# A hybrid encoder trunk: low parts of the mixers' weights read back from DRAM, the first weights in quarters beside x, and the mixer's steps in another order

## The chip, the cores and the metric

The kernel runs on one core of a Trainium2 chip. A time is the device time of one execution in microseconds (us). TensorE (PE) multiplies matrices, VectorE (DVE), ScalarE (ACT) and GpSimd (POOL) work on elements, and SyncE (SP) issues most of the DMAs. Each engine runs its own queue of instructions in order and waits for the others by semaphores.

## What is computed

x is 512 tokens of 1024 features, all float32. Two layers, each a half-step feed-forward, a mixer with three groups of heads, and another half-step feed-forward:

```python
for i in range(DEPTH):                       # DEPTH = 2
    x = x + 0.5 * swiglu(rmsnorm(x, ffn1_norm[i]), ffn1_w_gate[i], ffn1_w_up[i], ffn1_w_down[i])
    h = rmsnorm(x, mix_norm[i]) @ w_in[i]
    y_mla = mla_mixer(h[..., OFF_Q:OFF_KV], h[..., OFF_KV:OFF_KPE], h[..., OFF_KPE:OFF_CONV], ...)
    y_conv = conformer_conv_mixer(h[..., OFF_CONV:OFF_HY], ...)    # gate, 31 taps, layer norm, silu
    y_hy = hyena_mixer(h[..., OFF_HY:], ...)                       # short taps, two long convolutions by DFT
    y = concat([rmsnorm(y_mla, g[:e1]), rmsnorm(y_conv, g[e1:e2]), rmsnorm(y_hy, g[e2:])])
    x = x + y @ w_out[i]
    x = x + 0.5 * swiglu(rmsnorm(x, ffn2_norm[i]), ffn2_w_gate[i], ffn2_w_up[i], ffn2_w_down[i])
return rmsnorm(x, final_norm)
```

mla_mixer is latent attention with 8 heads: queries from a normalised 256-wide latent, keys and values from a 128-wide one, a rotary key of 32 features that all heads share, softmax over 512 keys.

## The kernel before

Everything is kept with features on the 128 partitions and the 512 tokens in the free dimension; x is eight such tiles. A float32 product is made of three passes on operands split into a high part (rounded to fp32r) and a low part (the rest): high x high, high x low, low x high. For a weight tile of 128 x 1024 this takes one load, a cast on ACT for the high part (a_copy, L360) and a subtraction for the low part (e_tt, on DVE at L371 or on POOL at L373), all in load_w; then 24 matmuls of 512 columns (mm3, L417 to L419). The raw, the high and the low part each take one of 13 buffers of 128 x 1024 (WBUFS, tag "w"). In the mixer four of these hold the tables of the long convolution's DFT.

The stages are: ffn, the first layer's first feed-forward (to about 395 us); the first mixer (to about 650 us); ffn_seven, the second feed-forward and the next layer's first one (other products, L692 to L694, with 256 columns); the second mixer (about 1332 to 1590 us); and a last ffn_seven. Between the tiles of ffn, pump calls a filler, early: rotary tables and the spectra of the long convolutions' filters for both layers, step by step; the second layer's spectra go to DRAM ("kept").

In the mixer, MIX_ORDER lists the steps: C (a projection pair of the gated convolution), A and B (its taps, one DVE operation each, on two halves of the channels), H (projections of the long convolution's inputs, with three short taps), Y (the ten steps of the two long convolutions), Q, KV and K (latents and the rotary key), W (the latent weights), V, S and P (values, scores and their products for each head), CF and HF (end of the convolution groups), OM and OR (the output projection, its attention half and the rest, eight tiles each; the later one of a tile also starts the next norm). A word's number after A, B, Y is a count. SECOND lists, for each step, which of its free choices (e_tt: DVE or POOL; e_scaled: ACT or POOL) take the second engine.

The kernel is written as a plan: every operation is put into it with an engine, a cost, what it reads and writes. A list scheduler (Plan.issue) then goes through modelled time and gives each free engine its ready operation with the lowest number (the order of the program), as far as buffers are free, tags being given out in the program's order. So the order of the words sets priorities, and the queue of each engine, SP with its loads included, is fixed by modelled time.

At the start, x's tiles come in turn with the parameters of layer 0 (67.5 KB) behind the first; the first weight pair comes in four half tiles (first_half), the first of them behind x[0], the second behind x[3], the others behind all of x. Gate and up products run one after the other over all eight x tiles.

## Time and profile before

| | us |
|---|---|
| three timed runs, median | 1943.11 |
| lowest and highest | 1941.32, 1943.93 |
| the profiled execution | 1942.71 |
| its span, first to last instruction | 1940.6 |

The profile of one execution gives, for every instruction, its engine, its start and length, and what ended the wait before it. A busy PE in it isn't a PE at its peak: matmuls are pipelined, and two that wait for each other can still cover the time between them. So beside the busy time the number of matmuls in a stretch is read, against the pace in a stretch where nothing waits. Over the whole span PE is busy 97%, DVE 78%, ACT 48%, POOL 24%.

### The profile page before, as it was taken

How to read it: one execution, taken by the hardware profiler on the slowest of the kernel's cores; microseconds unless marked ns; L12 is line 12 of the kernel's file. 1: busy time of each engine (PE TensorE's matmuls, PEld its weight loads, DVE VectorE, ACT ScalarE, POOL GpSimd, SP SyncE). 2: the span in 40 equal slices, each digit the busy share in tenths (PEclk: the TensorE clock that was granted, in tenths of full speed). 3: DMA queues.
4: the chain of work that ended last, by engine and by line, in shares of the span. 5: the costliest groups of instructions: out<-in, count | busy, mean ns of one | idle time of the engine just before them, and what ended most of it. 6: DMA issues, size and time to landing. Idle time of an engine off the chain costs nothing.

```text
span 1940.6 us, 28881 instructions
## 1 busy us (share of the span) xinstructions
PE 1890.0 (97%) x11265; PEld 1672.8 (86%) x11265; DVE 1506.1 (78%) x2323; ACT 932.3 (48%) x1533; POOL 465.5 (24%) x410
## 2 busy tenths in 40 slices
PE   9999999997999899999999999999999989999998
PEld 7888888886878899989889998997777879899898
DVE  7655465659998988869798886973899899688684
ACT  6333223433695644525454452543368675345253
POOL 1133103445465201001020000104466521000002
PEclk9999999999999999999999999999999999999999
DMA  6333333432003223323323232343310133323231
GB/s 218 101 102 102 121 109 100 129 113 76 12 17 101 90 88 109 110 87 109 109 88 104 93 120 77 109 153 103 98 33 17 45 104 100 118 87 116 81 131 44
DMA packets 61209, 185.52 MB, mean 96 GB/s; under 512 B 6928, under 2 KB 11024, under 8 KB 61072
## 3 DMA queue, kind: packets, MB, share of 16 engines
q1 hardware_dynamic: 57616, 176.86, 27.4%
q0 software_dynamic: 3456, 6.82, 1.2%
q8 instruction: 88, 1.44, 0.3%
q14 instruction: 49, 0.40, 0.1%
HBM read 179.45 MB, written 4.19 MB: 95 GB/s over the span
## 4 chain that ended last, share of the span: by engine, by line
PE 79%; DVE 9%; ACT 4%; DMA 4%; POOL 2%; issue 2%; POOLq 0%; SPq 0%; ACTq 0%; DVEq 0%
PE ps L419 15%; PE ps L417 15%; PE ps L418 15%; PE ps L692 11%; PE ps L694 10%; PE ps L693 10%; DMA wr<-in_win 1%; DVE ptl L333 1%; ACT wh L360 1%; POOL wl L373 1%; DMA wr<-in_dn 1%; DVE wl L371 1%; PE ps L408 1%; DMA wr<-in_gu 1%; ACT p L355 1%
## 5 line engine op out<-in xcount | busy, mean ns | idle before, releaser
L360 ACT CAST wh<-wr 128x1024 fp32r<-128x1024 f32 (+2 forms) x394 | 392.1, 1000 | 547.0 <-DMA wr<-in_gu 204.0
L371 DVE TENSOR_TENSOR wl<-wr,wh 128x1024 fp32r<-128x1024 f32 (+2 forms) x354 | 443.7, 1255 | 252.2 <-ACT wh L360 220.8
L694 PE MATMUL ps<-xa,wl 128*128 128x256 f32 x1320 | 373.9, 283 | 6.8 <-DVE wl L371 6.8
L692 PE MATMUL ps<-xa,wh 128*128 128x256 f32 x1320 | 374.6, 284 | 4.6 <-ACT wh L360 3.4
L693 PE MATMUL ps<-xa,wh 128*128 128x256 f32 x1320 | 373.5, 283 | 0.0
L373 POOL TENSOR_TENSOR s<-s,rb 128x256 f32<-128x256 f32 (+1 forms) x79 | 97.9, 1242 | 909.0 <-DVE s L333 769.3
L694 PEld LDWEIGHTS ps<-xa,wl 128*128 128x128 f32 x1320 | 253.2, 192 | 7.8 <-DVE wl L371 7.8
L692 PEld LDWEIGHTS ps<-xa,wh 128*128 128x128 f32 x1320 | 253.2, 192 | 7.0 <-ACT wh L360 3.8
L417 PE MATMUL ps<-gh,wh 128*128 128x512 f32 x656 | 255.4, 389 | 0.0
L418 PE MATMUL ps<-gl,wh 128*128 128x512 f32 x656 | 255.4, 389 | 0.0
L419 PE MATMUL ps<-gh,wl 128*128 128x512 f32 x656 | 255.2, 389 | 0.0
L693 PEld LDWEIGHTS ps<-xa,wh 128*128 128x128 f32 x1320 | 253.3, 192 | 0.4
L417 PE MATMUL ps<-xh,wh 128*128 128x512 f32 x544 | 215.1, 395 | 0.0
L418 PE MATMUL ps<-xl,wh 128*128 128x512 f32 x544 | 213.2, 392 | 0.0
L419 PE MATMUL ps<-xh,wl 128*128 128x512 f32 x544 | 212.9, 391 | 0.0
L419 PEld LDWEIGHTS ps<-gh,wl 128*128 128x128 f32 x656 | 123.1, 188 | 25.7
L418 PEld LDWEIGHTS ps<-gl,wh 128*128 128x128 f32 x656 | 123.2, 188 | 25.1
L417 PEld LDWEIGHTS ps<-gh,wh 128*128 128x128 f32 x656 | 123.2, 188 | 24.9
L419 PEld LDWEIGHTS ps<-xh,wl 128*128 128x128 f32 x544 | 103.0, 189 | 21.8
L417 PEld LDWEIGHTS ps<-xh,wh 128*128 128x128 f32 x544 | 103.3, 190 | 21.4 <-issue 0.2
L418 PEld LDWEIGHTS ps<-xl,wh 128*128 128x128 f32 x544 | 103.2, 190 | 21.4 <-issue 0.2
L355 ACT ACTIVATE s<-s 128x512 f32<-128x512 f32 x88 | 55.4, 632 | 128.6 <-DVE s L333 128.6
(305 smaller groups left out, 3915.5 us busy)
## 6 DMA issues: line engine op xcount, KB each, us to landing
wr<-in_gu SPq DMA_DIRECT2D x174, 512.0 KB, 3.6
wr<-in_dn SPq DMA_DIRECT2D x64, 512.0 KB, 3.7
wr<-in_win SPq DMA_DIRECT2D x28, 512.0 KB, 3.5
wr<-in_dn SPq DMA_DIRECT2D x32, 384.0 KB, 3.2
wr<-in_wout SPq DMA_DIRECT2D x32, 256.0 KB, 2.7
dft<-in_dft POOLq DMA_DIRECT2D x8, 448.0 KB, 4.7
x<-in_xT SPq DMA_DIRECT2D x8, 256.0 KB, 6.0
mat<-in_spec POOLq DMA_DIRECT2D x8, 256.0 KB, 3.7
```

Of the source, the lines that this page charges most:

```text
L333: lambda: nc.vector.tensor_tensor(out=g(o), in0=g(x0), in1=g(x1), op=op), rd(x0, x1), [o],
L355: lambda: nc.scalar.activation(g(o), g(x0), func, bias=g(bias), scale=g(scale), **({} if accum is None else {"accum_out": g(accum)})),
L360: plan.add("ACT", 0.06 + o.free * 0.86e-3, lambda: nc.scalar.copy(out=g(o), in_=g(x0)), rd(x0), [o])
L371: lambda: nc.vector.tensor_tensor(out=g(o), in0=g(x0), in1=g(x1), op=op), True),
L373: lambda: nc.gpsimd.tensor_tensor(out=g(o), in0=g(x0), in1=g(x1), op=op), True)],
L408: plan.add("PE", 0.11, lambda: nc.tensor.transpose(g(o), g(x0), g(ident)), [x0, ident], [o])
L417: nc.tensor.matmul(oo, lhsT=h, rhs=x0, start=(i == 0), stop=False)
L418: nc.tensor.matmul(oo, lhsT=h, rhs=x1, start=False, stop=False)
L419: nc.tensor.matmul(oo, lhsT=lo, rhs=x0, start=False, stop=(i == n - 1))
L692: nc.tensor.matmul(oo, lhsT=h, rhs=x0, start=start, stop=False, skip_group_check=more)
L693: nc.tensor.matmul(oo, lhsT=h, rhs=x1, start=False, stop=False, skip_group_check=more)
L694: nc.tensor.matmul(oo, lhsT=lo, rhs=x0, start=False, stop=stop, skip_group_check=more)
```

## The change

- keep_low, new: in the first feed-forward, beside the steps of the filter spectra, one or two weight tiles of the mixers at a time are loaded, split, and their low part is stored to DRAM: 13 of the 14 projection tiles (all but the rotary key's), the 3 latent tiles and the 8 output tiles of both layers, 48 of 512 KB in all.
- load_kept takes the place of load_w in the mixers: raw part and low part are both loaded, and only the cast for the high part is left. The output tiles are read in halves, as before.
- MIX_ORDER and SECOND are new, and BLOCKS and SIDES, the order of the blocks and sides of the long convolutions.
- The first weight pair comes in quarters, each with both gate and up for two of x's tiles, in turn with x; the gate and up products run side by side. The gain of the first norm is loaded by itself (4 KB); the parameters of layer 0 come behind x.

```diff
...
-BLOCKS = ((1, 0), (1, 0))
-SIDES = ((0, 1), (1, 0))
+BLOCKS = ((0, 1), (0, 1))
+SIDES = ((1, 0), (1, 0))
 SEVEN_CHUNKS = ((0, 6), (6, 14), (14, 22))
...
-MIX_ORDER = ("C0 A2 C1 A1 B1 H1 Q A1 B2 H2 H0 B2 A2 B2 A2 B2 Y1 KV K Y1 W H3 B4 A2 S0 B3 A6 S1 B1 H4 B1 H5 A1 B1 "
-             "A2 B2 A1 B2 Y1 B3 S4 Y2 A4 V A2 P4 S2 Y1 B2 A2 S5 B1 Y1 A2 B1 P2 S3 S6 S7 Y1 P0 P1 P3 P6 P5 P7 CF Y1 "
-             "OM0 OM2 Y1 HF OR0 OM4 OM1 OM7 OM5 OM6 OR1 OM3 OR2 OR3 OR4 OR5 OR6 OR7")
-
-SECOND = ("C0:12 K:0 C1:012 Q:134 H1:0 Y0:0123 H5:0 Y1:01347 Y2:01234567 KV:01 H2:0 H4:0 W:012 Y4:0 S2:23 S0:01 "
-          "Y5:012345 S1:012 Y7:0123567 S4:012 S5:4 S3:12 Y6:01234567 P1:0 S6:234 S7:0134 P3:01 P5:01 P7:0 "
-          "CF:0456 OM0:0 OM4:0 HF:01 OM3:0 OR0:0 OM6:0 OR1:467 OR2:03 OR3:0245 OR4:3 OR6:3 OR7:2")
+MIX_ORDER = ("C0 A5 K H0 C1 B1 A1 H1 H2 B1 A2 B1 A2 B2 A1 Y1 A1 KV B1 Q H4 Y1 W S0 B1 H3 A1 Y1 A1 H5 Y1 A2 B2 S2 "
+             "B2 S1 B2 A1 B1 A1 B1 A1 B2 A2 B1 A1 B1 S4 Y2 B1 V P0 B1 P1 A2 P2 A2 B1 P4 B1 A2 S3 A1 B1 A1 B1 Y1 S5 "
+             "B2 S6 S7 B2 Y1 B1 P3 Y1 P6 CF Y1 P5 P7 OM0 OM3 HF OM1 OR0 OM4 OR1 OM2 OR2 OR3 OR4 OM7 OM5 OR5 OM6 "
+             "OR6 OR7")
+
+SECOND = ("C1:0 Q:012 Y0:01235 KV:0 K:0 Y2:0123456 S0:024 S1:123 Y1:0123567 S4:014 Y4:0 Y3:0 S2:03 Y5:01234 "
+          "S5:124 Y7:12457 S3:03 S6:0134 S7:01234 Y6:0127 P3:1 P7:0 CF:023456 Y8:0 Y9:0 OR0:12 OR1:125 OR2:01 "
+          "OR3:456 OR4:012 OR5:356 OR6:2 OR7:347")
 SECOND = {w: set(map(int, n)) for w, n in (t.split(":") for t in SECOND.split())}
 POOL_OUT = (2,)
 SLOTS = 60
...
-    def mm3(o, pairs):
+    def mm3(o, pairs, first=True, last=True):
...
-                nc.tensor.matmul(oo, lhsT=h, rhs=x0, start=(i == 0), stop=False)
+                nc.tensor.matmul(oo, lhsT=h, rhs=x0, start=(first and i == 0), stop=False)
                 nc.tensor.matmul(oo, lhsT=h, rhs=x1, start=False, stop=False)
-                nc.tensor.matmul(oo, lhsT=lo, rhs=x0, start=False, stop=(i == n - 1))
+                nc.tensor.matmul(oo, lhsT=lo, rhs=x0, start=False, stop=(last and i == n - 1))
             return go
 
         for i, p in enumerate(pairs):
...
+    gain = const([P, KD], "gain")
...
     def pc(l, name, i=0, rows=P):
         c = PC[name] + i
+        if (l, name) == (0, "ffn1"):
+            return gain[:, i:i + 1]
         return par[l][:rows, c:c + 1]
 
 
...
+        return hi, lo
+
+    lows = {}
+
+    def keep_low(l, name, i, src):
+
+        raw, hi, lo = wtile("wr", F32), wtile("wh", F32R), wtile("wl", F32R)
+        load(raw, src)
+        a_copy(hi, raw)
+        e_tt(lo, raw, hi.f, ALU.subtract, 0)
+        t = lows[l, name, i] = plan.tile(dram, 32 * depth, "low", (P, 1024), F32, nm("low"))
+        load(t, lo.f)
+
+    def keep_lows(l):
+        for name, n in (("win", 14), ("wkvb", 1), ("wqb", 2), ("wout", KD)):
+            for i in range(n):
+                if name != "win" or i != 7:
+                    yield l, name, i, a[name][l] if name == "wkvb" else a[name][l, i]
+
+    def load_kept(l, name, i, c=slice(0, 1024)):
+
+        n = c.stop - c.start
+        raw, hi, lo = wtile("wr", F32), wtile("wh", F32R), wtile("wl", F32R)
+        src = a[name][l] if name == "wkvb" else a[name][l, i]
+        load(raw[:, :n], src[:, c])
+        load(lo[:, :n].f, lows[l, name, i][:, c])
+        a_copy(hi[:, :n], raw[:, :n])
         return hi, lo
 
     def ktiles(wt, n):
...
-        first_tiles = bool(first)
         for ci, (c0, c1) in enumerate(FF_CHUNKS):
             gh, gl = [], []
             for b in range(c0, c1):
                 p2 = []
-                for j in range(2):
-                    wt = first.pop() if first else load_w(a[f"gu{which}"][l, b, j], 1024)
+                if first and b == 0:
+                    p2 = [ps(), ps()]
+                    first(*p2)
+                for j in range(len(p2), 2):
+                    wt = load_w(a[f"gu{which}"][l, b, j], 1024)
                     p = ps()
                     mm3(p, nrm.pairs(wt))
                     p2.append(p)
                 gh.append(s2(F32R, "gh"))
                 gl.append(s2(F32R, "gl"))
                 held.append((*p2, gh[-1], gl[-1]))
-                if not (first_tiles and b == 0):
+                if not (first and b == 0):
                     for t in held:
                         evac(*t)
                     held.clear()
 
...
-            wt = load_w(a["win"][l, mt], 1024)
+            wt = load_kept(l, "win", mt)
...
-            lat["wkv"] = load_w(a["wkvb"][l], 1024)
-            lat["wq"] = [load_w(a["wqb"][l, k], 1024) for k in range(2)]
+            lat["wkv"] = load_kept(l, "wkvb", 0)
+            lat["wq"] = [load_kept(l, "wqb", k) for k in range(2)]
...
-            wt = load_w(a["wout"][l, d, :, 512:1024], 512)
+            wt = load_kept(l, "wout", d, slice(512, 1024))
...
-            wt = load_w(a["wout"][l, d, :, 0:512], 512)
+            wt = load_kept(l, "wout", d, slice(0, 512))
...
-    halves = [[s2(s="w0"), s2(F32R, "w0h"), s2(F32R, "w0l")] for _ in range(4)]
-
-    def first_half(i):
-        raw, hi, lo = halves[i]
-        load(raw, a["gu1"][0, 0, i // 2, :, (i % 2) * S:(i % 2 + 1) * S])
-        split(raw, hi, lo)
-
+    quarters = []
     load(x[0], a["xT"][0])
-    load(par[0], a["par"][0])
-    first_half(0)
+    load(gain, a["par"][0, :, 0:KD])
     for k in range(KD):
         if k:
             load(x[k], a["xT"][k])
+        if k % 2 == 0:
+            raw, hi, lo = s2(s="w0"), s2(F32R, "w0h"), s2(F32R, "w0l")
+            load(raw.halves(), a["gu1"][0, 0, :, :, k * P:(k + 2) * P].rearrange("j p c -> p j c"))
+            quarters.append((hi, lo))
         nrm.add(k, False)
-        if k == 3:
-            first_half(1)
-    first_half(2)
-    first_half(3)
-    load(cc, a["cc"])
-    load(ident, a["ident"])
-
-    class Halves:
-
-
-        def __init__(self, parts):
-            self.parts = parts
-
-        def __getitem__(self, k):
-            h, c = divmod(k[1].start, S)
-            return self.parts[h][:, c:c + P]
-
-    first = [tuple(Halves([halves[2 * j][i], halves[2 * j + 1][i]]) for i in (1, 2)) for j in (1, 0)]
+        if k % 2 == 0:
+            split(raw, hi, lo)
+    for t, n in ((par[0], a["par"][0]), (cc, a["cc"]), (ident, a["ident"])):
+        load(t, n)
+
+    def first(pg, pu):
+
+        for k in range(KD):
+            hi, lo = quarters[k // 2]
+            for j, p in enumerate((pg, pu)):
+                c = slice(j * 256 + k % 2 * P, j * 256 + k % 2 * P + P)
+                mm3(p, [(hi[:, c], lo[:, c], *nrm.x[k])], k == 0, k == KD - 1)
 
...
-        yield from spectra(0, specs[0])
-        for l in range(1, depth):
-            yield from spectra(l, specs[l])
+        todo = [lw for l in range(depth) for lw in keep_lows(l)]
+        steps = 0
+        for l in range(depth):
+            for _ in spectra(l, specs[l]):
+                steps += 1
+                for _ in range(1 + (steps % 4 != 0)):
+                    if todo:
+                        keep_low(*todo.pop(0))
+                yield 1
+            if l == 0:
+                continue
             for k in range(2):
                 for jb in range(2):
                     for o in range(2):
                         t = plan.tile(dram, 8 * (depth - 1), "kept", (P, S), F32, nm("kept"))
                         load(t, specs[l][k][jb][o])
                         specs[l][k][jb][o] = t
+        while todo:
+            keep_low(*todo.pop(0))
+            yield 1
```

## Rows read from the trace of the kernel before

**Rows 1.** First line of the page: the span.
```profile
span 1940.6 us, 28881 instructions
```
**Rows 2.** Busy time by stretch: from:to, length, engines' busy us (instructions), PEclk, DMA share, GB/s.
```profile
0.00:25.00 25.00, 21.24 (x74) 15.52 (x75) 18.33 (x27) 18.73 (x29) 1.41 (x10) 0.93 0.90 320
...
50.00:395.00 345.00, 345.00 (x1526) 285.38 (x1525) 195.20 (x266) 121.22 (x165) 88.89 (x76) 1.00 0.35 111
395.00:418.00 23.00, 23.00 (x111) 19.16 (x110) 8.96 (x18) 7.25 (x9) 10.68 (x6) 1.00 0.34 113
...
440.00:490.00 50.00, 39.44 (x167) 30.75 (x166) 46.72 (x71) 20.56 (x31) 27.71 (x21) 0.90 0.21 67
490.00:600.00 110.00, 108.05 (x593) 89.75 (x592) 102.72 (x206) 85.29 (x176) 62.06 (x64) 1.00 0.06 20
...
635.00:655.00 20.00, 15.05 (x112) 13.78 (x111) 19.52 (x36) 13.01 (x25) 4.71 (x4) 1.00 0.15 53
1330.00:1356.00 26.00, 23.70 (x102) 19.30 (x102) 5.78 (x9) 6.13 (x8) 12.45 (x8) 0.94 0.25 81
...
1378.00:1427.00 49.00, 42.28 (x181) 33.19 (x180) 46.21 (x73) 21.88 (x31) 29.30 (x21) 0.94 0.20 65
...
1572.00:1592.00 20.00, 15.06 (x109) 13.62 (x108) 19.97 (x38) 12.99 (x26) 4.26 (x5) 1.00 0.15 54
```
**Rows 3.** Waits of PE in the mixers (third of the second): total, times, longest us.
```profile
PE ps L417 <- ACT qh L360: 6.5, 1, 6.5
PE ps L408 <- DVE sq L371: 3.3, 1, 3.3
...
PE ps L408 <- POOL r L390: 2.5, 2, 2.3
```
**Rows 4.** Groups on DVE, 397 to 640 us: xcount | busy us, mean ns | idle before.
```profile
L371 DVE TENSOR_TENSOR wl<-wr,wh 128x512 fp32r<-128x512 f32 x9 | 6.2, 695 | 0.4 <-ACT wh L360 0.4
L371 DVE TENSOR_TENSOR wl<-wr,wh 128x1024 fp32r<-128x1024 f32 x5 | 6.1, 1219 | 5.0 <-ACT wh L360 5.0
...
L371 DVE TENSOR_TENSOR w<-m 128x256 f32<-128x256 f32 x3 | 4.4, 1479 | 0.0
...
L371 DVE TENSOR_TENSOR fold<-ho 128x128 f32<-128x128 f32 x2 | 2.4, 1216 | 0.0
...
L371 DVE TENSOR_TENSOR xr<-xr,xs 128x256 f32<-128x256 f32 x3 | 1.2, 413 | 0.0
```
**Rows 5.** Groups on POOL, 397 to 640 us, same columns.
```profile
L373 POOL TENSOR_TENSOR wl<-wr,wh 128x1024 fp32r<-128x1024 f32 x11 | 26.4, 2397 | 20.1 <-ACT wh L360 19.9 <-issue 0.2
...
L373 POOL TENSOR_TENSOR wl<-wr,wh 128x512 fp32r<-128x512 f32 x7 | 9.5, 1365 | 3.6 <-PE ps L418 3.4 <-issue 0.2
```
**Rows 6.** Timeline, 436 to 441 us: start us, length us, instruction.
```profile
436.44 0.29 DVE L371 TENSOR_TENSOR fold<-ho 128x128 f32<-128x128 f32 x1
...
438.22 2.40 POOL L373 TENSOR_TENSOR wl<-wr,wh 128x1024 fp32r<-128x1024 f32 x1 [6.13 <-ACT wh L360]
...
438.62 2.14 DVE L371 TENSOR_TENSOR fold<-ho 128x128 f32<-128x128 f32 x1
```
**Rows 7.** First feed-forward: DVE group, cast (ns), landing of loads, SP's wait.
```profile
L371 DVE TENSOR_TENSOR wl<-wr,wh 128x1024 fp32r<-128x1024 f32 x49 | 61.8, 1261 | 111.3 <-ACT wh L360 111.3
...
L360 ACT CAST wh<-wr x32: 836/1050/1057, 205.7 to 389.5; 128x1024 fp32r<-128x1024 f32 x24, 128x768 fp32r<-128x768 f32 x8
...
wr<-in_gu SPq DMA_DIRECT2D x31, 512.0 KB, 3.4
...
SPq L398 <- PE ps L419: 108.4, 21, 7.3
```
**Rows 8.** Timeline of the first tile: first matmul, last x tiles, next tile's first.
```profile
7.00 0.50 PE L417 MATMUL ps<-xh,w0h 128*128 128x512 f32 x1 [1.76 <-ACT w0h L360]
...
12.79 1.32 ACT L355 ACTIVATE xh<-x,par 128x512 fp32r<-128x512 f32 x2
...
20.93 0.19 PEld L417 LDWEIGHTS ps<-xh,wh 128*128 128x128 f32 x1
```

## The prediction

> **What bounds the kernel now.** The profiled execution took 1942.71 us, of which 1940.6 us are its span [rows 1]; the median of the three timed runs is 1943.11 us, so the sum below is made against 1942.7 and the 0.4 us between them is ignored. First come the busy times by stretch [rows 2]: the long feed-forward stretches keep TensorE (PE) full. From 50 to 395 us, 1526 matmuls take 345 us, 0.226 us each with nothing between them; I use that as the pace of a 512-column matmul, and one 128x1024 weight tile, 24 of them, is 5.42 us of PE. What PE loses lies in few places. In the first mixer, 440 to 490 holds 167 matmuls, worth 167 x 0.226 = 37.7 us of the 50, so 12.3 us are lost, a part of it to a granted clock of 0.90 behind the gaps. Then 490 to 600 shows 2.0 us idle (the matmuls there are short ones of several widths, so this row understates the loss) and 635 to 655, where the mixer gives over to the next feed-forward, 4.95 us. The second mixer repeats it: 26 - 102 x 0.226 = 2.9 us at 1330 to 1356, 49 - 181 x 0.226 = 8.1 us at 1378 to 1427, and 4.9 us at 1572 to 1592. So some 19 us can be seen in one mixer and 18 us in the other, and hardly anything outside them but the first tile.
>
> Why PE waits there: VectorE (DVE) is busy 46.72 of 50 us and 102.72 of 110 us in those stretches [rows 2], and the waits of PE [rows 3] name the queries' high part qh (6.5 us), a sum of squares on DVE (3.3 us), and in the second mixer the power r on GpSimd (POOL), 2.5 us. Up to 490 the mixers wait for the small chains that feed the first scores, through DVE and POOL queues that are full of other work. The loads are not what PE waits for.
>
> **The change part by part.**
>
> *Low parts read instead of computed.* In the mixer 13 projection tiles, 3 latent tiles and 16 half tiles no longer need their subtraction. By the assignment in the code before, POOL does 12 full and 7 half ones and DVE 4 full and 9 half ones; the rows show the same (of the five full ones on DVE in that stretch one belongs to the next feed-forward; POOL's twelfth begins before the stretch) [rows 4, 5]. DVE loses 4 x 1.22 + 9 x 0.695 = 11.1 us per mixer; POOL loses 26.4 + 9.5 = 35.9 us in the stretch shown. POOL's long subtractions also stretch DVE work: a 128x128 fold took 0.29 us alone and 2.14 us when it began 0.4 us after a 2.40 us subtraction on POOL, and it ended with that [rows 6]. Two folds (1216 against 290 ns) and three 128x256 sums (1479 against about 413 ns) are stretched by 1.9 + 3.2 = 5.1 us per mixer [rows 4]. I take this back in full, though other POOL work stays that can do the same.
>
> The Trainium skill, SBUF — State Buffer, section "Who interferes with whom", says that a DVE operation with two SBUF inputs and a GpSimd operation that reads SBUF take one shared port pair, and whoever starts first keeps it for its whole length while the other waits. Here the trace agrees (the fold ended 0.14 us after the subtraction). By that rule up to 35.9 us of blocked DVE time per mixer could come free where the rows show 5.1; this would carry the kernel to the third case below. It speaks against the change too, since the new table gives POOL other operations with the same port.
>
> *New choice of engine (SECOND).* Counted call by call: ten 512-wide, twelve 256-wide and one 128-wide operations go from DVE to POOL (12.2 us at 0.695, 0.413 and 0.29 us), eleven, five and one come back (10.0 us): 2.2 us less on DVE. But of what leaves, 4.4 us (nine 256-wide and one 512-wide) lie in the output projections at the end; ahead of them DVE gets 2.2 us more. Three probability scalings go from ScalarE (ACT) to POOL.
>
> *New order.* K comes second in place of after KV, KV and Q go ahead of the scores, and S0 is called with 18 convolution taps ahead of it instead of 23; H3 and H5 stand behind S0 as cover for PE (two tiles, 10.8 us). DVE is busy only 8.96 of the 23 us from 395 to 418 [rows 2]: the first tap waits for two projections and products queued behind a subtraction. With that gone I estimate that the taps begin some 4 us earlier. So DVE, up to the end of the convolution and the attention, comes out ahead by 4.9 (full subtractions) + 5.1 + 4 - 2.2 = 11.8 us per mixer. That is what the mixers can win where DVE is the bound, and it nearly covers the losses there. I take back 8 of the 12.3 us in the first and 7.5 of the 11.0 us in the second mixer, 2.5 us in each of the stretches behind, and 2 of the 5 us in each tail, where DVE loses nine half subtractions: 8 + 7.5 + 5 + 4 = **24.5 us**. The bounds: at least 4 us per mixer (the full subtractions less the 2.2, and little from unstretching), at most all that the rows show, 12.3 + 11.0 + 4 + 10 = 37 us. P's and the swapped blocks and sides of the long convolution cost the same work in another order.
>
> Each mixer tile now takes two loads, so 2 x 0.52 MB per 5.42 us, 195 GB/s, for nine free weight buffers (13 less the 4 of the transform's tables). A low part takes its buffer at the load, some 2 us sooner than before, while the raw part's is free after the cast. I cost this at nothing: the cover is the tile before it on PE; if it is gone, each tile waits 1 to 2 us.
>
> *Making the low parts.* 48 times in the first feed-forward: a 512 KB load, a cast, a subtraction of 1.26 us on DVE and a 512 KB store, for which I take the 3.4 us of a load of that size (between half and twice that) [rows 7]. DVE is busy 195 of 345 us there [rows 2]; 48 x 1.26 = 60 us fit. The store stands in SP's queue and waits for DVE, and behind it wait the loads of the feed-forward. SP already waits for buffers freed by PE for 108 us of that stretch [rows 7], which is to say that loads are issued as early as buffers allow. In buffer time: a feed-forward tile holds its three for about 6.5 + 7.7 + 6.7 = 21 us, a kept one for some 13.5 us (estimates from the same load, cast and subtraction); two of the one and 1.8 of the other per 10.8 us are 66 of 13 x 10.8 = 140 buffer us. So the lead shrinks from four tiles to some two or three, and PE should stay fed. I charge **+2 us** for single late chains (between 0 and the fourth case below).
>
> *First tile.* Its weights come in four pieces, one for each two tiles of x, both products run side by side, and a 4 KB gain is loaded ahead in place of the 67.5 KB of parameters. Now PE's first matmul starts at 7.00, the last two x tiles are scaled from 12.79 on and the next tile starts at 20.93 [rows 8]. The 48 matmuls are 48 x 0.226 = 10.8 us, so 3.1 us are lost; but the granted clock of the first 25 us is 0.93 [rows 2], so a part of that goes with a start at the lower of its two levels (1.2 for 2.4 GHz). The last x tile now has 1 MB of weights in front of it instead of 0.5 MB, about 1 to 2 us later, but only 12 matmuls per two tiles (2.7 us) wait for it. Gain 0 to 2.5, taken **1.5 us**.
>
> Sum: 1942.7 - 24.5 - 1.5 + 2 = **1919 us** (1918.7).
>
> **The rivals.**
> 1. *The forecast*, 1919 us, by itself 1909 to 1929.
> 2. *DVE stays the bound.* Its work ahead of the output projections falls only by 4.9 - 2.2 us, POOL's other work stretches as before, and the waits move from Q's squares to another chain. For it speaks that DVE is at 93% from 440 to 600. 4 us per mixer and 1 us at the first tile, less 2 us in the feed-forward: 1942.7 - 8 - 1 + 2 = 1936.
> 3. *The mixers become bound by PE.* All 37 us and 2.5 us at the start come back, nothing is lost: 1903. For it: the small chains were late mostly by POOL and DVE queues that get free; against it: DVE still has about 200 of 245 us of work.
> 4. *Slower: the first feed-forward loses its lead.* If the kept tiles take the buffers, a tile's chain is load 3.4, cast 1.05, subtraction 1.26, and one kept subtraction of 1.26 ahead in the DVE queue: 7.0 us against 5.42, 1.55 us lost. On each tile behind a kept pair, 27 of them: 42 us, so 1919 - 2 + 42 = 1959. It decides from 26 us on, that is where the loss is 1 us per such tile. Against it: the buffer count above, half used.
> 5. *No effect*: the subtractions were hidden on POOL, and the new order only moves PE's gaps; two loads per tile bring a new wait of the size of what is won: 1943.
>
> **How the numbers follow.** Chances: 0.50, 0.20, 0.14, 0.09, 0.07. Faster by over 0.2%, which is about what a measurement of this kernel can tell (4 us), are the first three: 0.84; within it the fifth: 0.07; slower the fourth: 0.09. The range leaves out the fourth and the fifth and reaches to the edge of the second and the third: 1900 to 1939.
>
> **What would show it.** Right: from 50 to 395 PE keeps 0.226 us per matmul with DVE at about 255 of 345 us; the second tile starts at about 19.4; between K's and S0's chains PE's waits for qh, for the squares and for r fall below 4 us in sum; POOL shows no 2.4 us subtraction in the mixers; the mixer ends 10 to 12 us earlier against the feed-forward before it. Wrong: PE gaps in the first feed-forward named by a load or a cast; PE waiting in the mixer for a load of a low part; a DVE still over 93% busy with the same total gaps.

## The result, and the profile after

| | us |
|---|---|
| kernel before, median (lowest to highest) | 1943.52 (1941.32 to 1944.12) |
| changed kernel, median (lowest to highest) | 1907.97 (1906.33 to 1911.68) |
| ratio, 95% interval | 0.9822 [0.9805, 0.9839] |
| profiled execution of the changed kernel | 1907.37 |

The change takes 35 us off, 1.8%. The forecast was 1919 us, in a range of 1900 to 1939: sign and range held, and the kernel gained 11 us more than forecast.

The head of the page after: span, then busy us, share of the span and instructions of each engine.

```profile
span 1905.6 us, 29281 instructions
...
PE 1881.2 (99%) x11265; PEld 1667.9 (88%) x11265; DVE 1554.1 (82%) x2333; ACT 975.0 (51%) x1575; POOL 419.4 (22%) x390
```

PE has the same 11265 matmuls as before, in a span 35.0 us shorter. DVE is busier in all (the 48 new subtractions in the first feed-forward), POOL less.

Where the 35.0 us went is read from the starts of PE's matmuls in the two traces. The marks are the last product with a down matrix ahead of each mixer, the first gate product behind it, at which the mixer counts as over, and the first product with a down matrix after that.

| stretch | before | after | difference | forecast |
|---|---|---|---|---|
| start to the end of the first feed-forward | 394.9 | 393.5 | -1.4 | -1.5 + 2 |
| first mixer, to the next gate product | 241.3 | 229.7 | -11.6 | -10.5 |
| from there to the first down product (its tail among six tiles) | 64.7 | 61.2 | -3.5 | -2 |
| the feed-forwards between the mixers | 635.3 | 633.0 | -2.3 | 0 |
| second mixer | 238.0 | 225.9 | -12.1 | -10 |
| its tail, among six tiles | 85.0 | 80.6 | -4.4 | -2 |
| the rest | 281.4 | 281.8 | +0.4 | 0 |

The stretches of after that answer to those of [rows 2], in the same columns (from:to, length, then busy us and instructions of PE, weight loads, DVE, ACT and POOL, then PE's granted clock, DMA share and GB/s):

```profile
0.00:25.00 25.00, 22.46 (x81) 17.70 (x82) 19.19 (x27) 18.93 (x29) 1.41 (x10) 1.00 0.91 327
...
50.00:395.00 345.00, 344.96 (x1526) 285.37 (x1525) 264.19 (x312) 165.84 (x211) 102.65 (x75) 1.00 0.73 252
...
440.00:490.00 50.00, 48.89 (x226) 39.34 (x226) 49.56 (x84) 25.18 (x40) 23.76 (x24) 1.00 0.39 123
488.60:598.60 110.00, 107.30 (x590) 88.79 (x590) 100.33 (x199) 83.22 (x172) 54.98 (x57) 1.00 0.16 52
622.00:642.00 20.00, 19.60 (x147) 18.05 (x146) 19.35 (x31) 14.23 (x26) 9.04 (x8) 1.00 0.25 80
...
1361.00:1410.00 49.00, 47.96 (x223) 38.65 (x222) 48.56 (x83) 25.06 (x40) 23.67 (x24) 1.00 0.39 124
...
1541.00:1561.00 20.00, 19.88 (x149) 18.57 (x148) 19.36 (x31) 14.11 (x26) 9.30 (x8) 1.00 0.25 80
```

The first feed-forward holds the same 1526 matmuls in 345 us as before, with DVE busy 264 us in place of 195 and twice the DMA traffic. In the mixers' set-up stretches 226 matmuls stand where 167 stood, and 223 where 181 stood, at a full clock: at 0.226 us each they fill the 50 and the 49 us. Both tails, taken from 1 to 2 us ahead of the gate product as in [rows 2], went from 5 us idle in 20 to 0.4 and 0.1, with 147 and 149 matmuls in place of 112 and 109. In the stretch behind the first set-up nothing was won: in the same 110 us, counted from the mixer's start, PE is idle 2.7 with 590 matmuls, where it was idle 2.0 with 593.

The waits of PE from 390 to 690 us, the first mixer (total, times, longest us):

```profile
PE ps L420 <- POOL ql L374: 0.8, 3, 0.4
PE ps L418 <- ACT qh L361: 0.7, 1, 0.7
PE ps L409 <- DVE fold L372: 0.4, 1, 0.4
PE ps L409 <- POOL sq L374: 0.4, 1, 0.4
```

The single waits of 6.5 and 3.3 us of [rows 3] are gone. Line numbers are some lines on: the free operation of DVE is L372, of POOL L374, ACT's cast L361, the three passes L418 to L420.

### The profile page after: what moved, and what is told of

It is laid out like the page before. It is cut to its first block, busy times and chain, and to the rows that moved or that the text cites. A ratio compares the mean times of both kernels' runs of the same rounds, so it can differ in the third digit from the quotient of the medians.

```text
span 1905.6 us, 29281 instructions
## 1 busy us (share of the span) xinstructions
PE 1881.2 (99%) x11265; PEld 1667.9 (88%) x11265; DVE 1554.1 (82%) x2333; ACT 975.0 (51%) x1575; POOL 419.4 (22%) x390
## 4 chain that ended last, share of the span: by engine, by line
PE 84%; DVE 9%; ACT 3%; DMA 2%; issue 1%; POOL 0%; POOLq 0%; SPq 0%; ACTq 0%; DVEq 0%
PE ps L418 16%; PE ps L420 16%; PE ps L419 16%; PE ps L725 11%; PE ps L726 11%; PE ps L727 11%; DVE ps L346 2%; PE ps L409 1%; DVE mx L1155 1%; DMA wr<-in_gu 1%; PE ps L434 1%; PE ps L433 1%; DVE m L334 1%; ACT wh L361 1%; DMA wr<-in_dn 1%
## 5 line engine op out<-in xcount | busy, mean ns | idle before, releaser
L361 ACT CAST wh<-wr 128x1024 fp32r<-128x1024 f32 (+2 forms) x442 | 442.1, 1005 | 506.1 <-DMA wr<-in_gu 148.7
L372 DVE TENSOR_TENSOR wl<-wr,wh 128x1024 fp32r<-128x1024 f32 (+1 forms) x376 | 492.3, 1312 | 161.3 <-ACT wh L361 128.1
L374 POOL TENSOR_TENSOR s<-s,rb 128x256 f32<-128x256 f32 (+1 forms) x79 | 105.1, 1333 | 898.5 <-DVE s L334 755.9
L418 PE MATMUL ps<-gh,wh 128*128 128x512 f32 x656 | 255.4, 389 | 0.0
L420 PE MATMUL ps<-gh,wl 128*128 128x512 f32 x656 | 255.2, 389 | 0.0
L418 PE MATMUL ps<-xh,wh 128*128 128x512 f32 x544 | 214.1, 394 | 0.3 <-ACT wh L361 0.3
L420 PE MATMUL ps<-xh,wl 128*128 128x512 f32 x544 | 211.9, 390 | 0.0
L420 PEld LDWEIGHTS ps<-gh,wl 128*128 128x128 f32 x656 | 123.2, 188 | 25.6
L418 PEld LDWEIGHTS ps<-gh,wh 128*128 128x128 f32 x656 | 123.2, 188 | 25.1
L418 PEld LDWEIGHTS ps<-xh,wh 128*128 128x128 f32 x544 | 102.2, 188 | 22.3 <-ACT wh L361 1.1
L420 PEld LDWEIGHTS ps<-xh,wl 128*128 128x128 f32 x544 | 102.1, 188 | 21.6
```

What stands on the lines that cost most here:

```text
L361: plan.add("ACT", 0.06 + o.free * 0.86e-3, lambda: nc.scalar.copy(out=g(o), in_=g(x0)), rd(x0), [o])
L372: lambda: nc.vector.tensor_tensor(out=g(o), in0=g(x0), in1=g(x1), op=op), True),
L374: lambda: nc.gpsimd.tensor_tensor(out=g(o), in0=g(x0), in1=g(x1), op=op), True)],
L418: nc.tensor.matmul(oo, lhsT=h, rhs=x0, start=(first and i == 0), stop=False)
L420: nc.tensor.matmul(oo, lhsT=lo, rhs=x0, start=False, stop=(last and i == n - 1))
```

## The experiments

A difference from the kernel before can be read directly. "Against the change" below is the difference of a run's ratio and 0.9822, times 1943 us, good to some 4 us by the intervals. What is said of a stretch of a run comes from its one profiled execution, by the marks above. In all kernels but the two last, every engine's queue follows anew from the edited program, since a list scheduler makes it; the two last leave the queues of the changed kernel as they are.

| kernel | median us | ratio to before, 95% | against the change |
|---|---|---|---|
| e1_order: new order, low parts still computed | 1988.78 | 1.0253 [1.0239, 1.0267] | +84 |
| e2_lows: kept low parts, old order | 1940.82 | 1.0001 [0.9991, 1.0011] | +35 |
| e3_start: quarters alone | 1938.17 | 0.9991 [0.9982, 1.0000] | +33 |
| e4_made: low parts made, not used | 1945.76 | 1.0033 [1.0021, 1.0046] | +41 |
| f1_poolhere: POOL's low parts computed again | 1953.05 | 1.0055 [1.0040, 1.0070] | +45 |
| f2_dvehere: DVE's low parts computed again | 1948.96 | 1.0031 [1.0018, 1.0044] | +41 |
| g1_cover_ahead: cover tiles ahead of S0 | 1929.11 | 0.9934 [0.9917, 0.9950] | +22 |
| e7_words: old choice of engines | 1947.21 | 1.0022 [1.0011, 1.0033] | +39 |
| n1_neutral_p3: one choice moved to a like step | 1924.96 | 0.9923 [0.9904, 0.9942] | +20 |
| n2_neutral_c0: another | 1943.89 | 1.0017 [1.0006, 1.0027] | +38 |
| h1_dve_fixed: f2, queues kept | 1929.35 | 0.9939 [0.9921, 0.9958] | +23 |
| h2_pool_fixed: f1, queues kept | 1958.44 | 1.0092 [1.0074, 1.0110] | +52 |

### One part alone

**The order alone.** MIX_ORDER, BLOCKS, SIDES and SECOND are the new ones; nothing is kept, and each low part is computed in the mixer on the engine that did it before. The first tile is as before.

```diff
+        if True:
+            a_copy(hi[:, :n], raw[:, :n])
+            low_here(lo[:, :n], raw[:, :n], hi[:, :n], on_pool(name, i, c))
+            return hi, lo
         load(lo[:, :n].f, lows[l, name, i][:, c])
...
-        todo = [lw for l in range(depth) for lw in keep_lows(l)]
+        todo = []
```

Here low_here is the subtraction, on DVE (L334) or on POOL (L365).

> The kernel before with the new order and the new choice of engines alone: the low parts are subtracted in the mixer as before, on the engine that did each before, nothing is kept in DRAM, the first tile is as before. My theory (the low parts relieve DVE and POOL, the order lays the score chains ahead and covers them; both are needed): a third of the 31.6 us that the two mixers win in the changed kernel, so 8 to 14 us faster, about 1932. Rival A (the order does nearly all, the subtractions were hidden): 25 to 32 us faster, about 1914. Rival B (the low parts do nearly all): within 4 us of before, 1940 to 1947.

Measured: 49 us slower than before, which no theory had. PE's waits in its first mixer:

```profile
PE ps L420 <- DVE wl L334: 11.5, 3, 5.4
PE ps L420 <- POOL wl L365: 7.0, 2, 5.9
PE ps L409 <- POOL sq L374: 4.3, 3, 2.1
```

PE waits for the low parts themselves, 18.5 us in one mixer. The new order has K second, KV and Q early, and a low part that is still to be computed behind other work comes too late for it. Without the kept low parts this order, in the queues that the scheduler makes of it, is worse than the old one.

**The kept low parts alone.** Old order, blocks, sides and first tile; SECOND is the old one without the entries of the subtractions that are gone. Against the kernel before, with keep_low and load_kept as in the change (lines cut at "..."):

```diff
-SECOND = ("C0:12 K:0 C1:012 Q:134 H1:0 Y0:0123 ...
+SECOND = ("C0:0 K:0 C1:0 Q:12 Y0:0123 ...
...
-            wt = load_w(a["win"][l, mt], 1024)
+            wt = load_kept(l, "win", mt)
```

> The kernel before with the low parts kept and read back alone: the order of the steps and the engines of all other operations are those of before, the first tile is as before. My theory: half of the mixers' 31.6 us, 14 to 20 us faster, about 1926. Rival A (order): within 4 us of before. Rival B (low parts): 25 to 32 us faster, about 1914.

Measured: no difference from before (0.9991 to 1.0011). Its waits of PE and its stretches in the first mixer (columns as above):

```profile
PE ps L417 <- ACT qh L360: 5.9, 1, 5.9
PE ps L408 <- POOL sq L373: 3.0, 1, 3.0
```

```profile
440.00:490.00 50.00, 44.00 (x194) 35.20 (x194) 47.46 (x78) 23.91 (x38) 18.07 (x17) 0.93 0.35 116
490.00:600.00 110.00, 104.69 (x573) 86.37 (x572) 94.70 (x192) 82.30 (x169) 54.43 (x59) 0.99 0.13 44
```

From 440 to 600 POOL is 17 us less busy than in [rows 2] and DVE 7. By 490 PE is ahead (194 matmuls in place of 167), but from 490 to 600 it falls back (573 in place of 593, with 5.3 us idle in place of 2.0). The wait for qh is almost as long as in [rows 3], and the one of 3.0 us is for another sum of squares, on POOL. With both queues freer some chains are still late in the old order; the place at which the order calls them may be the cause, but this run doesn't show it. As run, neither part brings anything by itself, and the two together bring over 30 us.

**The quarters alone**, on the kernel before.

```diff
+        if k % 2 == 0:
+            raw, hi, lo = s2(s="w0"), s2(F32R, "w0h"), s2(F32R, "w0l")
+            load(raw.halves(), a["gu1"][0, 0, :, :, k * P:(k + 2) * P].rearrange("j p c -> p j c"))
```

> The kernel before with the first tile's weights in quarters beside x, and the gain by itself, and nothing else of the change. My theory: the next tile starts 1.5 us earlier (19.7 us) and all behind it follows, since PE has no slack up to the mixer: 1 to 2 us faster, about 1942. Rival: the gain is lost again at the first wait of the mixer, whose parts come by loads and DVE work: no difference.

Measured: 1.9 us faster, at the edge of its interval; its first feed-forward ends at 392.4 us in place of 394.9. The changed kernel's own first tile, from its timeline (start us, length us, instruction):

```profile
6.75 0.80 PE L418 MATMUL ps<-xh,w0h 128*128 128x512 f32 x1 [1.10 <-ACT w0h L361]
...
14.10 0.71 ACT L356 ACTIVATE xh<-x,gain 128x512 fp32r<-128x512 f32 x1
...
19.44 0.19 PEld L418 LDWEIGHTS ps<-xh,wh 128*128 128x128 f32 x1
```

Against [rows 8] PE begins 0.25 us sooner, the last of x has been scaled 0.7 us later (by 14.81; the two of [rows 8] by 14.11), and the second tile begins 1.5 us sooner, at 19.44 (forecast 19.4).

**The making alone.** The low parts are made and stored in the first feed-forward, but the mixers, in the old order, compute theirs again and read none.

```diff
+        if True:
+            a_copy(hi[:, :n], raw[:, :n])
+            low_here(lo[:, :n], raw[:, :n], hi[:, :n], on_pool(name, i, c))
+            return hi, lo
         load(lo[:, :n].f, lows[l, name, i][:, c])
```

> The kernel before with the low parts made and stored in the first feed-forward as in the change, but not used: the mixers subtract as before. Theory of the prediction: 0 to 4 us slower, 2 in the sum. By the trace of the changed kernel, in which the stretch from 50 to 395 us holds the same 1526 matmuls: no difference, 1942 to 1945, and the first mixer starts at the same time. Rival (the buffers' lead is lost where this work stands): 26 us slower or more.

Measured: 5.7 us slower than before, more than forecast. In the profiled execution 3.5 of it lie in the first feed-forward, which ends at 398.4, and 3.0 in the first mixer, where PE waits 5.1 us for the squares in place of 3.3 [rows 3]. In the feed-forward PE waits at one place, in the chain of the filter spectra. Its timeline, the DMA group of 248 to 258 us (count, KB each, median us from issue to landing), and PE behind the wait (columns as above):

```profile
257.02 1.05 ACT L360 CAST wh<-wr 128x1024 fp32r<-128x1024 f32 x1 [0.97 <-DMA wr<-in_dn]
...
257.97 0.61 ACT L360 CAST hp<-hdn 128x512 fp32r<-128x512 f32 x1
258.10 1.23 DVE L371 TENSOR_TENSOR wl<-wr,wh 128x1024 fp32r<-128x1024 f32 x1 [0.98 <-ACT wh L360]
259.36 0.69 DVE L333 TENSOR_TENSOR hp<-hdn,hp 64x512 fp32r<-64x512 f32 x1
...
260.10 0.50 PE L405 MATMUL ps<-hp,fwh 128*128 128x512 f32 x1 [2.12 <-DVE hp L333]
```

```profile
wr<-in_dn SPq DMA_DIRECT2D x3, 512.0 KB, 5.6
```

```profile
262.00:264.00 2.00, 2.00 (x6) 1.62 (x5) 1.72 (x3) 0.50 (x1) 0.00 (x0) 0.50 0.47 100
```

Weights of the feed-forward itself land late, a median of 5.6 us after their issue in place of some 3.4 [rows 7], among the stores and loads of the kept tiles. The cast on ACT and the subtraction on DVE of one of them stand ahead of the two small operations hp, which PE needs sooner than the weight, and PE waits 2.12 us. Behind the gap the granted clock is 0.50, the lower level, up to about 264, and some nine matmuls start 0.43 us apart in place of 0.226. So the clock behind the gap costs nearly as much again as the gap. In the changed kernel the same chain comes 3 us earlier and nothing waits. So the making can cost some us, by where one late load falls in the queues, or nothing.

### One part undone, the queues made anew

Each edits the changed kernel. f1 computes the 19 low parts per mixer that POOL did before (12 full, 7 half) on POOL again, f2 the 13 of DVE on DVE; the others are still read.

```diff
+        if on_pool(name, i, c):          # f2: if not on_pool(name, i, c)
+            a_copy(hi[:, :n], raw[:, :n])
+            low_here(lo[:, :n], raw[:, :n], hi[:, :n], on_pool(name, i, c))
+            return hi, lo
         load(lo[:, :n].f, lows[l, name, i][:, c])
```

> The changed kernel, but the 19 low parts per mixer that POOL subtracted in the kernel before (12 full, 7 half) are subtracted there again, on POOL; the other 13 are read. Theory 1, after the first four runs (with the new order PE waits for the low parts themselves, and POOL's 2.4 us ones come latest): 15 to 40 us slower than the changed kernel, 1923 to 1948, with PE waiting for wl of POOL. Theory 2, that of the prediction (DVE is the bound, POOL's subtractions cost only by stretching DVE, 5 us per mixer): about 10 us slower, 1918.

> The changed kernel, but the 13 low parts per mixer that DVE subtracted in the kernel before (4 full, 9 half) are subtracted there again, on DVE; the other 19 are read. Theory 1 (the low parts' delay counts, and DVE's come earlier): 2 to 10 us slower than the changed kernel, 1910 to 1918. Theory 2 (DVE is the bound): 11 us per mixer back, 1926 to 1930.

Measured: +45 and +41 us against the change, each above its forecasts and more than the whole gain. Both can't be shares of the gain: the sum would be 86 of 35. f2's longest wait of PE is for one low part of an output half, and ends at 630.3 us:

```profile
PE ps L420 <- DVE wl L334: 5.1, 1, 5.1
```

Two more parts were undone: the cover (H3 and H5 ahead of S0, so that no tile of theirs stands between its chains), and the choice of engines (e7: the old SECOND as in e2, the new order).

```diff
-"C0 A5 ... KV B1 Q H4 Y1 W S0 B1 H3 A1 Y1 A1 H5 Y1 A2 B2 S2 "
+"C0 A5 ... KV B1 Q H4 H3 H5 Y1 W S0 B1 A1 Y1 A1 Y1 A2 B2 S2 "
```

> The changed kernel with H3 and H5 called ahead of the first scores (Q H4 H3 H5 Y1 W S0 in place of Q H4 Y1 W S0 B1 H3 A1 Y1 A1 H5): K and the latents stay early, but no projection's matmuls stand in PE's queue between the queries' product and the scores that need it. Theory 1 (the order wins by cover): the wait for qh is back, 5 to 7 us per mixer, 1918 to 1922. Rival (it wins by K and the latents being early, the cover counts for little): 1906 to 1912.

> The changed kernel with the choice of engines of the kernel before (its indices without those of the subtractions that are gone): the order of the steps and the low parts read are those of the change. Theory 1 (order and low parts win, the choice of engines little): 2 to 8 us slower than the changed kernel, 1910 to 1916. Rival (the new table carries a large part, since DVE is the bound and 2.2 us per mixer net of it and its places matter): 15 us slower or more, 1923 on.

Measured: +22, above both of its ranges, and +39 us. g1 shows what a missing cover does, PE waiting for the queries' own chains:

```profile
PE ps L420 <- POOL ql L374: 3.9, 5, 1.9
PE ps L418 <- ACT qh L361: 2.9, 3, 1.7
```

But every part that was undone costs 20 to 45 us, and that raises the question of what is measured: the part, or the new queues around it.

### Edits that are worth nothing

Two edits of SECOND move one operation to the other engine in one step, and one of the same kind back in another. n2 is not quite worth nothing: by its own expectation it starts the first taps about 1 us later.

```diff
n1: -P3:1 P7:0    +P5:1 P7:0
n2: -SECOND = ("C1:0 Q:012    +SECOND = ("C0:0 Q:012
```

> The changed kernel with one entry of the choice of engines moved: of two equal 512-wide sums of squares in the values' steps, P5's goes to POOL in place of P3's. The work of every engine is the same. Theory 1 (the queues are fitted to one another, so that any other choice costs, whatever its work; then undoing one part of the change at a time doesn't price that part): 6 to 20 us slower than the changed kernel, 1914 to 1928. Theory 2 (what the four runs before lost is the price of the part undone): within 4 us of the changed kernel, 1904 to 1912.

> The changed kernel with one entry of the choice of engines moved: the gate's product of the first half of the convolution's channels is made on POOL and that of the second half on DVE, the reverse of the change. The work of every engine is the same; the taps of the first half begin about 1 us later. Theory 1 (fitted queues): 15 to 35 us slower than the changed kernel, 1923 to 1943. Theory 2: within 4 us, 1904 to 1912.

Measured: +20 and +38 us (17 and 36 by the plain difference of the medians, which leaves out that the kernel before differs by 3 us between the chips). Every engine has as many instructions as in the changed kernel. So 20 to 38 us can be lost by the new fit of the queues, and the +22 to +45 of g1, e7, f1 and f2 don't price their parts. The same holds for e1, e2 and e4, whose queues are new as well.

Where the time is lost differs. n1 loses 7.7 and 8.8 us in the two tails and only 0.3 and 0.6 in the mixers ahead of them; n2 loses 12.0 and 9.1 in the mixers, 6.8 and 8.9 in the tails. n1's first tail, which answers to 622 to 642 of the changed kernel:

```profile
625.00:645.00 20.00, 13.39 (x78) 12.19 (x77) 17.62 (x28) 10.08 (x21) 7.79 (x8) 0.74 0.16 54
```

PE stands idle 6.6 us there and runs at a granted clock of 0.74, with 78 matmuls for 147. g1 is the other way round: 9.7 and 10.6 us in the mixers, where the cover was taken away, and nothing in the tails. That fits a price of the cover, but doesn't prove one, since n2 loses as much in the same place.

### The queues kept

The 13 (h1) or 19 (h2) low parts are computed in the mixer with every other instruction where it stands in the changed kernel: the load of the low part leaves SP's queue, but the scheduler still reckons with it, and the subtraction goes behind the cast of its tile in the order of issue.

```diff
+        if on_pool(name, i, c):          # h1: if not on_pool(name, i, c)
+            plan.add("SP", 4 * P * n / 355e3 + 0.01, lambda: None, [lows[l, name, i]], [lo], late=1.95)
...
+            def both():
+                nc.scalar.copy(out=g(h), in_=g(x0))
+                on.tensor_tensor(out=g(o), in0=g(x0), in1=g(h.f), op=ALU.subtract)
+
+            plan.add("ACT", 0.06 + n * 0.86e-3, both, [x0], [h])
+            return hi, lo
         load(lo[:, :n].f, lows[l, name, i][:, c])
```

In the traces PE, DVE, ACT and POOL run the changed kernel's instructions in its order, with 26 subtractions more on DVE in h1 and 38 more on POOL in h2.

> The changed kernel with the order of every engine's queue kept as it is, PE's above all, and with the 13 low parts per mixer that DVE subtracted before subtracted on DVE again right behind their cast, the load of the low part left out. So 11.1 us of DVE work per mixer come back into a fixed order. Theory of the prediction (DVE is the bound): 8 to 11 us per mixer, 1924 to 1930. Theory 1 (fitted queues; the work itself is a small part): 2 to 6 us per mixer, 1912 to 1920.

> As the run before, but for the 19 low parts per mixer that POOL subtracted before: some 36 us of POOL work per mixer come back into a fixed order, DVE's queue stays as it is. Theory of the prediction (they cost by stretching DVE, 5.1 us per mixer): 1916 to 1920. Rival (POOL's long operations delay its own short ones, and PE waits for those): 10 to 20 us per mixer, 1928 to 1948.

h1 measured: +23 us, by the starts of the matmuls 13.5 in the first mixer with its tail and 11.1 in the second. The subtractions themselves were forecast as 11.1 us of DVE per mixer: DVE's work comes back nearly one for one, as one would expect where DVE is at 49.56 of 50 us. The theory by which little would be lost once the queues are kept falls here.

h2 measured: +52 us, above both forecasts, 24.8 and 27.6 in the two mixers with their tails. PE's waits in the first:

```profile
PE ps L409 <- POOL fold L374: 5.8, 2, 4.7
PE ps L409 <- POOL sq L374: 4.4, 2, 4.0
PE ps L420 <- POOL ql L374: 2.8, 2, 2.1
PE ps L420 <- POOL wl L509: 1.7, 1, 1.7
```

PE waits mostly for POOL's own short operations, not for the low parts (wl). The two longest of these waits in its timeline:

```profile
452.13 2.35 POOL L509 TENSOR_TENSOR wl<-wr,wh 128x1024 fp32r<-128x1024 f32 x1 [2.17 <-ACT wh L508]
...
454.43 0.52 POOL L374 TENSOR_TENSOR fold<-ho 128x128 f32<-128x128 f32 x1
...
455.01 0.90 PE L409 MATMUL ps<-ident,fold 128*128 128x128 f32 x3 [4.67 <-POOL fold L374]
```

```profile
475.13 2.35 POOL L509 TENSOR_TENSOR wl<-wr,wh 128x1024 fp32r<-128x1024 f32 x1 [1.66 <-ACT wh L508]
...
477.44 1.71 POOL L374 TENSOR_TENSOR sq<-sq,sq 128x512 f32<-128x512 f32 x1
...
479.21 1.11 PE L409 MATMUL ps<-ident,sq 128*128 128x128 f32 x4 [3.97 <-POOL sq L374]
```

A fold of 0.52 us stands behind a subtraction of 2.35, which itself has let POOL wait 2.17 us for its cast; PE waits 4.67 us for the fold. The group of the full subtractions from 393 to 640 us (busy us, mean ns, idle before them):

```profile
L509 POOL TENSOR_TENSOR wl<-wr,wh 128x1024 fp32r<-128x1024 f32 x12 | 28.6, 2387 | 37.2 <-ACT wh L508 37.2
```

They occupy POOL's queue for 28.6 us and block it, waiting for casts, for up to 37.2 more. In these 50 us from 440 DVE is not short: it is busy 40.76 us, while PE has 173 matmuls at a clock of 0.90, as in the kernel before.

```profile
440.00:490.00 50.00, 40.25 (x173) 32.49 (x172) 40.76 (x61) 16.21 (x23) 23.76 (x16) 0.90 0.25 84
```

Over the first mixer with its tail DVE is stretched as well. Its busy time before, in the changed kernel and in h2:

```profile
394.90:700.87 305.97, 288.51 (x1617) 246.57 (x1615) 273.64 (x475) 182.07 (x333) 137.15 (x119) 0.98 0.21 66
393.51:684.37 290.86, 286.45 (x1616) 244.59 (x1615) 261.74 (x457) 180.28 (x330) 108.41 (x110) 1.00 0.35 111
394.79:710.47 315.68, 293.15 (x1617) 248.11 (x1615) 272.33 (x458) 180.61 (x330) 150.18 (x130) 0.98 0.23 78
```

With the same instructions in the same order DVE is busy 10.6 us longer in h2 than in the changed kernel, and 10.1 in the second mixer.

What h1 and h2 price is the subtractions put into queues that were made without them. It is not their share of the gain: the two come to 75 of 35.

## Why the prediction was right, and where its sizes were not

- **What bounds the kernel.** Right as to the place: 31.6 of the 35.0 us come from the mixers and their tails, and the single waits that it named are gone. As to the cause, small chains behind full DVE and POOL queues, h1 and h2 bear it out in the new order; in the old order freer queues alone (e2) left the wait for qh at 5.9 us.
- **Where in the mixers.** 8 and 7.5 us were taken for the set-up stretches and 2.5 for each stretch behind. All came in the set-up: 59 matmuls more in the first, worth 13 us at 0.226 us each, against some 1 us lost behind it. There the prediction took 2.5 us of the 2.0 idle that its row shows, and PE is now idle 2.7.
- **The low parts on DVE.** Right in size: 11.1 us of work per mixer, 11 to 13.5 us of time in h1. In the set-up the room was filled with work that came later before: DVE is now busy 49.56 of 50 us there, with PE full. The prediction named a DVE "still over 93% busy with the same total gaps" as a sign of failure; only the gaps count.
- **The stretching of DVE.** 5.1 us per mixer were taken back in full, and nothing of it shows. DVE's busy time fell by 11.9 and 9.0 us per mixer with its tail, which the low parts (11.1) account for alone; with the 2.2 of the new choice of engines its terms came to 18.4.
- **The low parts on POOL.** This is the other mis-sized term. Only the stretching was taken for it. In the new queues these subtractions, put back, cost some 26 us per mixer (h2): DVE is stretched by 10, and, since POOL takes its queue in order, short operations that PE waits for stand behind subtractions of 2.4 us that wait for casts. The row that showed it was in hand: [rows 5] has 19.9 us of POOL idle for ACT's casts in front of its full subtractions. The prediction counted how long they run, not how long they hold the queue.
- **Adding up parts.** The sum took the order and the low parts as terms that add. They don't: e1 +49 us, e2 0, both about -33 (the 35 less the 1.9 of e3). The new order needs the low parts ready at the load (e1, h1, h2). Why the freed queues bring nothing in the old order (e2) is not shown: the place of its chains, or the fit of its new queues. "P's and the swapped blocks and sides cost the same work in another order" was true of the work; where operations fall decides 20 to 38 us with the same work (n1, n2). That "2.2 us less on DVE" for the choice of engines was a count of work too.
- **The tails.** 2 us each were taken of 5; 3.5 and 4.4 came. The bound for it (all that the rows show) would have been nearer, as for the set-up stretches, where by the count of matmuls nothing is lost any more.
- **Making the low parts.** DVE was forecast at about 255 of 345 us and is at 264: its full subtractions of the first feed-forward, old and new, take 1377 ns in place of 1261 [rows 7]. Nothing of it reaches PE. The charge of 2 us lies between what the changed kernel (none) and e4 (3.5 us there) show. The fourth rival, a feed-forward that loses its lead, did not come; e4's one late load is all that was seen of it.
- **First tile.** Right: 1.5 forecast, 1.5 at the start of the second tile, 1.4 at the end of the first feed-forward, 1.9 in e3's time.
- **Not foreseen:** 2.3 us between the mixers, where the change edits nothing. Over all kernels here this stretch takes 632.7 to 635.4 us, with no relation to a part that I could find; it stays open.
- **The signs named.** The waits for qh, squares and r in the first mixer sum to under 2 us (forecast under 4); POOL has no 2.4 us subtraction left in the mixers; the mixers end 11.6 and 12.1 us earlier (forecast 10 to 12).
- **How much was luck.** The prediction had no term for the fit of the new queues. n1 and n2 have every part of the change and one small operation moved, and take 1925 and 1944 us; n2 would have been outside the range and no faster than before. Within the sum terms missed both ways: the set-ups and the tails brought more than was taken, the stretches behind the set-ups nothing, and the making cost nothing in the first feed-forward.

The third rival, mixers bound by PE at 1903, was closer to the time than the forecast (5 us against 11): in its set-up stretches the changed kernel has reached what it described. PE is still idle 3.8 us in the first mixer (12.5 before), 2.7 of them from 488.6 to 598.6. What remains open is which moves of the new order (K early, the cover, P's among the taps) do most: with the queues made anew by every edit, the runs can't tell, and moving single steps in kept queues was not tried; nor was the new choice of engines with the old order.

## What to carry to other kernels

An operation on a queue that is taken in order costs its length and also the time it waits at the head; look at what stands behind it and who waits for that, before pricing it by its busy time. Parts of a change to a kernel whose queues are fitted to one another need not add, and undoing one of them with the queues made anew measures the fit along with it: first run an edit that is worth nothing, see in which stretch it loses, and price a part with all other instructions kept in place. Such a price holds for those queues; it is not a share of the gain. A resource that stays 95% busy after a change says nothing; count the matmuls in the stretch.

## What the runs showed of the hardware

The DMA traffic of the first feed-forward more than doubled, to a share of 0.73 and 252 GB/s, and the loads landed later. The changed kernel's groups from 50 to 395 us, DVE's kept and other subtractions, and DMAs with median us from issue to landing:

```profile
L372 DVE TENSOR_TENSOR wl<-wr,wh 128x1024 fp32r<-128x1024 f32 x95 | 130.3, 1377 | 53.7 <-ACT wh L361 52.8
```

```profile
low<-wl SPq DMA_DIRECT2D x45, 512.0 KB, 4.7
...
wr<-in_gu SPq DMA_DIRECT2D x32, 512.0 KB, 4.9
```

```profile
SPq L399 <- DVE wl L372: 133.9, 49, 6.7
SPq L399 <- PE ps L420: 40.2, 14, 6.6
```

A 512 KB load took 4.9 us in place of 3.4 [rows 7], a store 4.7; SP waited 133.9 us for DVE with its stores, and loads behind them in its queue waited too. None of that reached PE: before, 108 us of SP's waiting was for buffers in use [rows 7], so there was lead to lose.

In h2 a DVE operation that takes 0.75 us in the changed kernel took 2.51 us, begun at 468.49, 0.44 us behind a subtraction of 2.40 us on POOL; it ended 0.55 us after that.

```profile
468.05 2.40 POOL L509 TENSOR_TENSOR wl<-wr,wh 128x1024 fp32r<-128x1024 f32 x1 [2.30 <-ACT wh L508]
468.49 2.51 DVE L346 SCALAR_TENSOR_TENSOR hkv<-hkv,par,rb 128x512 f32<-128x512 f32 x1 [0.60 <-ACT rb L361]
```

This agrees with the Trainium skill, SBUF — State Buffer, section "Who interferes with whom", by which the one that starts first keeps the shared port pair for its whole length. The blocking itself is real here, some 10 us of DVE's time per mixer in h2, but not what PE mainly waited for: DVE was busy 40.76 of 50 us in that stretch, and PE's longest waits were for POOL's queue.
